# A hybrid decoder layer on one core: convolution taps, sample products and the scaling of x put on the vector engine, and one evacuation and sigmoid moved up

## The chip, the core and the metric

The kernel runs on one core of a Trainium2 chip. The core has a matrix engine (TensorE, PE in the profile, with its weight loads shown as PEld), a vector engine (VectorE, DVE), a scalar engine (ScalarE, ACT), a general engine (GpSimd, POOL) and a queue engine that starts transfers (SyncE, SP). Each engine runs its own instructions in program order and waits on semaphores for the others. The metric is the device time of one execution in microseconds (us).

## The reference

One inference step of a one-layer decoder over 1024 prompt positions and 8 x 8 sample positions, width 1024, in float32. All 1088 positions go through the same layer, laid out with channels on the 128 partitions and positions along the free dimension.

```python
h = rmsnorm(x, norm_mix_pre)
(a_b, a_c, a_u, b_p, c_q, c_f, c_i, c_g, d_a, d_g) = split(h @ w_in, 10)   # ten blocks of 256 channels
ya = a_b * conv3(a_c * a_u)                       # A: short causal convolution
yb = scale * W_grp(mean_w(b_p) - b_p)             # B: trailing means over 2, 4, 8, 16 positions
yc = headnorm(hgrn2(c_q, c_f, c_i)) * silu(c_g)   # C: gated recurrence, done in chunks
u  = d_a * sigmoid(d_g)                           # D: gate, then a causal convolution of width 31
yd = silu(layernorm(conv31(u) + conf_b))
x  = x + rmsnorm(concat(ya, yb, yc, yd) @ w_out)
x  = x + rmsnorm(swiglu(rmsnorm(x)))
```

The kernel also returns the updated states of the four mixers. For the prompt the convolutions begin with zeros, for the samples with a given state.

## The kernel before, in words

**Products in split precision.** Every float32 operand of a product is split into a high part (a cast) and a low part (the rest): `XH[k]`, `XL[k]` for the activations, two halves of a tile `wop` for the weights. Each product is three products: high by high, low by high and high by low. `split_w` (lines 137 to 140) makes the cast on ACT (L139) and the rest on DVE (a `TT` at L65).

**Units.** `h @ w_in` is done in 20 units of 128 output columns. One unit is 8 slices k of the width by 3 products by 3 column chunks `CH` of 256, 384 and 448 positions, so 72 matmuls; its result lies in 3 of the 6 banks of PSUM. Line 203 gives the order of the units: `UNITS = (12, 10, 8, 18, 16, 13, 19, 11, 9, 17, 4, 2, 6, 0, 5, 3, 7, 1, 14, 15)`. `U0` to `U4` are the first five.

**The opening (lines 254 to 340)** is written out by hand for ACT, DVE and PE. Units 12, 10 and 8 (`U0`, `U1`, `U2`) run on x that is not yet divided by its root mean square, while the squares for that root are summed. The reciprocal roots are spread over the partitions into the tile `rb0` (L298). Then the loop of lines 324 to 335 rewrites the eight slices of x: `scale_x(k)` scales slice k by the gain and `rb0` and casts it into `XH[k]`, and `low_x(k)` makes `XL[k]`. For k = 6 and 7 the multiplication with `rb0` is done by POOL (lines 322 and 323); for the others by one DVE instruction (`STT`, L71). In the same loop stand `prep_half(U3, ...)`, which splits the weights of unit 18, and `evac_r(U1)` and `evac_r(U2)`, which multiply the results of units 10 and 8 with `rb0` on their way out of PSUM. Unit 18 needs the three banks of unit 10. `HF[0]` is the forget gate of mixer C for the first 128 channels; its sigmoid stands at line 339, behind the loop.

**The planned part (lines 345 to 1128).** From unit 18 on a planner in Python writes the instruction order of PE and DVE; the order of ACT, POOL and SP is left to the compiler's scheduler. `unit` yields after 4 or 8 matmuls, `drive` turns that into a budget (0.1135 per matmul), and `hook` spends it on generators that yield what they cost: first the handlers of finished units (`first`), then the recurrence of mixer C (`crit`, function `hgrn`), then the rest (`bulk`). A generator that yields nothing is passed over for that time. Tiles are counted out with `take` and `give` (`z` and `u` have two buffers each). At the start of unit 18 the budget is set to -12.

**The wide convolution.** `d_gate` and `d_val` make u; `d_conv(j)` convolves channels 128 j to 128 j + 127. For the 64 sample positions it multiplies windows of u with the 31 taps on POOL, four products for each of two halves `q`, and sums them with a DVE reduction (L529). For the 1024 prompt positions 21 taps are multiply-adds on DVE (L71, `y<-u,taps,y` in the profile; the first is a `tensor_scalar`). The other 10 (`OFF`) are products on ACT (L540, `y<-u,taps`) into staging tiles, each of which but the first is added to `acc` by a transfer that accumulates (L542, `y<-y`), started from POOL. At the end DVE adds `acc` (line 551). `a_c`, the short convolution, and `b_pool`, the pooling, use tiles that the staging also uses, and wait for `("acc", j)`.

**Behind it.** `d_fin` does the layer norm of mixer D after both `d_conv`. `put_y` writes the mixers' outputs into `XH` and `XL` while the last unit runs, mixer D's first. Then come the output projection (`project`, matmuls at L1189), the feed-forward part (L1461 and others) and the outputs.

Of the kernel before, what the change touches and what calls it, by code (L numbers as in the profile page):

```python
# [12 lines left out]
AF = mybir.ActivationFunctionType  # L13
ALU = mybir.AluOpType
# [4 lines left out]
SEQ = 1024  # L19
# [33 lines left out]
def body(ctx, tc, xT, win, wout, wgu, wdn, par, con, msk, poolw, s_conv, s_pool, s_hgrn, s_conf,  # L53
         yT, o_conv_p, o_pool_p, o_hgrn_p, o_conf_p, o_conv_s, o_pool_s, o_hgrn_s, o_conf_s, hd, hx):
    nc = tc.nc
    V, S, PE, GP, SY = nc.vector, nc.scalar, nc.tensor, nc.gpsimd, nc.sync
# [7 lines left out]
    def TT(out, a, b, op=ALU.mult, eng=None):  # L64
        (eng or V).tensor_tensor(out, a, b, op)  # L65
# [4 lines left out]
    def STT(out, a, s, b, op0=ALU.mult, op1=ALU.add, eng=None):  # L70
        (eng or V).scalar_tensor_tensor(out=out, in0=a, scalar=s, in1=b, op0=op0, op1=op1)  # L71

    def f32(ap):
        return ap.bitcast(F32)
# [15 lines left out]
    def pc(name, i):  # L90
        return prm[:, PCOL[name] + i:PCOL[name] + i + 1]
# [6 lines left out]
    XH = [T(xp, [P, NT], f"xh{k}", F32R) for k in range(KT)]  # L98
    XL = [T(xp, [P, NT], f"xl{k}", F32R) for k in range(KT)]
# [70 lines left out]
    ys = [T(yp, [P, NT], f"y{k}") for k in range(KT)]  # L170
# [76 lines left out]
    def prep_half(n, h):  # L247
        hl = T(wp, [P, 2, 4 * P], "wop", F32R).rearrange("p w (k c) -> p w k c", c=P)
        split_w(wraw[n][h], hl)
        wq.setdefault(n, []).append(hl)  # L250
# [3 lines left out]
    with tc.manual_schedule(engines={mybir.EngineType.Activation, mybir.EngineType.DVE, mybir.EngineType.PE}):  # L254
        sq = {}
        pu[U0], pu[U1] = banks(), banks()

        def square(k):
            sq[k] = ht(NT)
            S.activation(sq[k], ys[k], AF.Square)  # L260
            if k:
                TT(sq[0], sq[0], sq[k], ALU.add)

        prep_half(U0, 0)
        for k in range(KT):
            split_x(k, pc("g_mix", k), CH if k == 0 else [(0, NT)])
            if k == 1:
                prep_half(U0, 1)
            if k in (2, 5):
                prep_half(U1, k // 5)  # L270
            if k >= 1:
                square(k - 1)
            mm_unit(U0, k)
            if k >= 3:
                mm_unit(U1, k - 3)
        square(KT - 1)
        zv.append(zt())
        for c, (o, n) in enumerate(CH):
            S.copy(zv[0][:, o:o + n], pu[U0][c][:, :n])
        st = sm()  # L280
        V.memset(st[64:, 8:9], 1.0)
        for i, (go, gn) in enumerate(GRP):
            PE.matmul(st[:gn, i:i + 1], sq[0][:, go:go + gn], ones[:, :1], start=True, stop=True, skip_group_check=True)
        mm_unit(U1, 5)
        for r0 in rsqrt_steps(st[:, :9], [P, 9], 1.0 / D, "x"):
            pass
        prep_half(U2, 0)
        prep_half(U2, 1)
        load_unit(U3)
        mm_unit(U1, 6)  # L290
        pu[U2] = banks()
        rb0 = ht(NT)
        for c, (o, n) in enumerate(CH):
            ps = sm()
            for i, (go, gn) in enumerate(GRP):
                if o <= go < o + n:
                    bcast(ps, r0[:, i:i + 1], gn, go - o)
            S.copy(rb0[:, o:o + n], ps[:, :n])  # L298
            if c == 1:
                mm_unit(U1, 7)  # L300
        mm_unit(U2, *range(KT))

        def scale_x(k):
            if k >= 6:
                S.activation(XH[k], ys[k], AF.Copy, scale=pc("g_mix", k))
            else:
                STT(ys[k], ys[k], pc("g_mix", k), rb0, ALU.mult, ALU.mult)
                S.copy(XH[k], ys[k])

        def low_x(k):  # L310
            if k >= 6:
                STT(XL[k], ys[k], pc("g_mix", k), f32(XH[k]), ALU.mult, ALU.subtract)
            else:
                TT(XL[k], ys[k], f32(XH[k]), ALU.subtract)

        def evac_r(n):
            t = ht()
            for c, (o, w) in enumerate(CH):
                TT(t[:, o:o + w], pu[n][c][:, :w], rb0[:, o:o + w])
            return t  # L320

        for k in (6, 7):
            TT(ys[k], ys[k], rb0, eng=GP)
        for k in range(KT):
            scale_x(k)
            if k >= 1:
                low_x(k - 1)
            if k in (1, 2):
                prep_half(U3, k - 1)
            if k == 3:  # L330
                HF[0] = evac_r(U1)
            if k == 4:
                load_unit(U4)
            if k == 6:
                HQ[0] = evac_r(U2)
        low_x(KT - 1)
        prep_half(U4, 0)
        prep_half(U4, 1)
        S.activation(HF[0], HF[0], AF.Sigmoid)
        S.activation(HQ[0], HQ[0], AF.Silu)  # L340


# [77 lines left out]
    done = set()  # L420

    def after(name):
        while name not in done:
            yield None

    def wait(n=1):
        for _ in range(n):
            yield None
# [51 lines left out]

    sg, uu = {}, {}
    US = 30 + SEQ
    OFF = 10

    def d_gate(j, ps):
        yield from take(z=1)
# [27 lines left out]
    def d_conv(j):  # L514
        u = uu[j]
        y = ys[6 + j]
        us = u[:, US:].rearrange("p (b t) -> p b t", t=38)
        dwj = taps[:, 31 * j:31 * (j + 1)]
        dwb = dwj.unsqueeze(1).unsqueeze(1).to_broadcast([P, 1, 8, 31])
        for q in range(2):  # L520
            yield from take(z=1)
            t = zt([P, 4 * 8, 31])
            for b in range(4):
                seg = us[:, q * 4 + b, :]
                win_ap = bass.AP(seg.tensor, seg.offset, [list(seg.ap[0]), [1, 8], [1, 31]])
                TT(t[:, b * 8:(b + 1) * 8], win_ap, dwb[:, 0], eng=GP)
            yield from wait(5)
            r = T(const, [P, 32], "cr")
            V.tensor_reduce(r, t, AX.X, ALU.add)  # L529
            TS(y[:, SEQ + 32 * q:SEQ + 32 * (q + 1)], r, pc("cb", j), 0.0, ALU.add, ALU.add)  # L530
            give(z=1)
            yield 1.4

        acc, *stage = [ys[i][:, :SEQ] for i in ((0, 1, 2) if j == 0 else (3, 5))]
        own = 31 - OFF
        for w in range(31):
            i = w // 2
            if w % 2 == 0 and i < OFF:
                dst = stage[i % len(stage)] if i else acc
                S.activation(dst, u[:, own + i:own + i + SEQ], AF.Copy, scale=dwj[:, own + i:own + i + 1])  # L540
                if i:
                    GP.dma_start(acc, dst, accum_op=ALU.add)  # L542
            if w >= own:
                continue
            if w == 0:
                TS(y[:, :SEQ], u[:, 0:SEQ], dwj[:, 0:1], pc("cb", j))
            else:
                STT(y[:, :SEQ], u[:, w:w + SEQ], dwj[:, w:w + 1], y[:, :SEQ])
            yield 1.2
        yield from wait(2 * LW)  # L550
        TT(y[:, :SEQ], y[:, :SEQ], acc, ALU.add)
        done.add(("acc", j))
        yield 1.2
        give(u=1)
        done.add(("conv", j))

# [47 lines left out]
        give(mm=3)  # L604

    def a_c(j, ps):
        yield from after(("acc", 0))
        while j not in zu:
            yield from wait(LW)
        yield from take(u=1)  # L610
        cu = ut(2 + SEQ + NB * 10)
        z = zu[j]
        cs = cu[:, 2 + SEQ:].rearrange("p (b t) -> p b t", t=10)
        GP.memset(cu[:, 0:2], 0.0)
        SY.dma_start(cs[:, :, 0:2], s_conv[j])
        yield from wait(LW)
        for (o, n), q in pchunks(ps):
            TT(cu[:, 2 + o:2 + o + n], q, z[:, o:o + n])
            yield 0.5
        TT(cs[:, :, 2:10], sample(ps), z[:, SEQ:].rearrange("p (b t) -> p b t", t=8))  # L620
        give(mm=3, z=1)
        SY.dma_start(o_conv_p[j], cu[:, SEQ:SEQ + 2])
        SY.dma_start(o_conv_s[j], cs[:, :, 8:10])
        y = ys[j]
        yb = y[:, SEQ:].rearrange("p (b t) -> p b t", t=8)
        for w in range(3):
            cw = pc("conv_w", 3 * j + w)
            if w == 0:
                S.activation(y[:, :SEQ], cu[:, 0:SEQ], AF.Copy, scale=cw)
                S.activation(yb, cs[:, :, 0:8], AF.Copy, scale=cw)  # L630
                yield from wait(LW)
            else:
                STT(y[:, :SEQ], cu[:, w:w + SEQ], cw, y[:, :SEQ])
                STT(yb, cs[:, :, w:w + 8], cw, yb)
                yield 1.4
        give(u=1)
        done.add(("conv a", j))
# [25 lines left out]
        bulk.insert(0, b_pool(j, p, s))  # L663

    def b_pool(j, p, s):
        yield from after(("acc", j))
        yield from wait(2 * LW)
        yield from take(h=2)

# [1281 lines left out]
```

## Time and profile before

| | us |
|---|---|
| runs | 1214.53, 1216.1, 1218.18 (median 1216.1) |
| the profiled execution, its own time | 1219.45 |
| its span in the profile | 1217.7 |
| PE busy | 1161.2 |
| DVE busy | 882.5 |
| ACT busy | 477.3 |
| POOL busy | 139.4 |

The span runs from the first to the last recorded instruction. A busy time is a sum over the whole span, which has stages with different limits: the opening, the planned part to about 381 us, and the projection and feed-forward parts behind it. The list of waits tells for each engine and line how long it sat idle and what ended that; a time given there for an engine that is not needed soon costs nothing. The tables by window give the busy time of each engine in a stretch, and as PEclk the clock granted to PE as a share of its full speed.

### The profile page before, as it was taken

The numbers are of one execution on the slowest core, as the hardware profiler recorded it, in microseconds if no ns is written. First come the engines' busy times: TensorE is split into PE (matmuls) and PEld (weight loads), VectorE is DVE, ScalarE is ACT, GpSimd is POOL, SyncE is SP. The second block draws the span as 40 slices with busy tenths as digits, with TensorE's granted clock in tenths as the row PEclk, the third lists the DMA queues.
The fourth block names the chain that finished last, engine by engine and source line by source line (L and its number), as shares of the span: only waits on it lengthen the run. The fifth ranks groups of instructions, "written<-read, shape, count | busy, mean of one in ns | idle before, by whom it ended". The sixth has DMA issues, their size and how long they took to land.

```text
span 1217.7 us, 21870 instructions
## 1 busy us (share of the span) xinstructions
PE 1161.2 (95%) x8435; PEld 1126.5 (93%) x8435; DVE 882.5 (72%) x1791; ACT 477.3 (39%) x1013; POOL 139.4 (11%) x206
## 2 busy tenths in 40 slices
PE   7899898599999999999999999999999999999995
PEld 6788888599899999999999999999999999999995
DVE  7775597379747567878766777877867558888666
ACT  7264532335226445343333444443433542222321
POOL 1202102200000000000000000000000332337323
PEclk9899899799979999999999999999999999999997
DMA  7116414630205412303313435533544678863555
GB/s 256 35 35 126 87 35 93 123 64 19 45 23 168 156 38 73 129 24 101 117 58 105 138 102 175 172 113 121 181 157 125 206 234 255 265 186 107 163 105 95
DMA packets 106057, 146.35 MB, mean 120 GB/s; under 512 B 25312, under 2 KB 72672, under 8 KB 105952
## 3 DMA queue, kind: packets, MB, share of 16 engines
q1 hardware_dynamic: 95008, 108.71, 28.9%
q0 software_dynamic: 10944, 36.25, 12.5%
q8 instruction: 66, 1.08, 0.4%
q14 instruction: 39, 0.32, 0.1%
HBM read 94.90 MB, written 40.57 MB: 111 GB/s over the span
## 4 chain that ended last, share of the span: by engine, by line
PE 80%; DMA 8%; DVE 6%; issue 2%; ACT 2%; POOL 1%; SPq 0%; ACTq 0%; POOLq 0%; DVEq 0%
PE p L1461 30%; PE p L1694 14%; PE mm L1052 11%; PE p L1189 8%; DMA y<-y 6%; PE p L1571 6%; PE p L1370 6%; PE mm L146 2%; DVE y L71 2%; PE sm L866 1%; DVE wop L65 1%; DMA raw<-wgu 1%; PE sm L437 1%; PE p L1155 0%; DMA y<-xT 0%
## 5 line engine op out<-in xcount | busy, mean ns | idle before, releaser
L65 DVE TENSOR_TENSOR wop<-raw,wop 128x512 fp32r<-128x512 f32 (+2 forms) x296 | 196.0, 675 | 98.7 <-ACT wop L1075 91.6
L1075 ACT CAST wop<-raw 128x512 fp32r<-128x512 f32 (+1 forms) x240 | 141.9, 604 | 244.3 <-DVE raw L65 115.8
L1461 PE MATMUL p<-xh,wop 128*128 128x272 f32 x1216 | 235.6, 289 | 1.7 <-DVE c L65 1.7
L1461 PEld LDWEIGHTS p<-xh,wop 128*128 128x128 f32 x1216 | 193.1, 188 | 1.9 <-DVE c L65 1.9
L1052 PE MATMUL mm<-xh,wop 128*128 128x256 f32 (+2 forms) x816 | 177.3, 346 | 16.1 <-ACT z L477 11.0
L1461 PE MATMUL p<-t,wop 128*128 128x272 f32 x912 | 177.2, 288 | 0.0
L1461 PE MATMUL p<-xl,wop 128*128 128x272 f32 x608 | 175.0, 288 | 0.0
L1052 PEld LDWEIGHTS mm<-xh,wop 128*128 128x128 f32 x816 | 137.3, 198 | 23.8 <-ACT z L477 11.4
L1461 PEld LDWEIGHTS p<-t,wop 128*128 128x128 f32 x912 | 144.7, 188 | 0.0
L1461 PE MATMUL p<-x,wop 128*128 128x272 f32 x456 | 130.5, 286 | 0.0
L1461 PEld LDWEIGHTS p<-xl,wop 128*128 128x128 f32 x608 | 114.6, 188 | 0.0
L1189 PE MATMUL p<-xh,wop 128*128 128x272 f32 x512 | 99.1, 290 | 0.0
L1052 PE MATMUL mm<-xl,wop 128*128 128x256 f32 (+2 forms) x408 | 97.6, 349 | 0.0
L1461 PEld LDWEIGHTS p<-x,wop 128*128 128x128 f32 x456 | 85.8, 188 | 0.0
L1694 PE MATMUL p<-xh,wop 128*128 128x272 f32 x456 | 82.0, 288 | 0.0
L1694 PE MATMUL p<-xl,wop 128*128 128x272 f32 x456 | 81.4, 288 | 0.0
L1189 PEld LDWEIGHTS p<-xh,wop 128*128 128x128 f32 x512 | 81.0, 188 | 0.0
L65 DVE TENSOR_TENSOR raw<-raw,raw 128x512 f32<-128x512 f32 (+1 forms) x123 | 71.2, 589 | 11.4 <-DMA raw<-wgu 8.7
L65 POOL TENSOR_TENSOR x<-raw,x 128x544 fp32r<-128x544 f32 (+3 forms) x6 | 7.5, 1246 | 605.5 <-ACT x L1619 575.1
L1189 PE MATMUL p<-xl,wop 128*128 128x272 f32 x256 | 74.0, 289 | 2.0 <-DVE xl L65 2.0
L1370 PE MATMUL p<-xh,wop 128*128 128x272 f32 x384 | 74.1, 289 | 0.0
L1052 PEld LDWEIGHTS mm<-xl,wop 128*128 128x128 f32 x408 | 69.6, 200 | 3.2 <-issue 0.4
(317 smaller groups left out, 2141.4 us busy)
## 6 DMA issues: line engine op xcount, KB each, us to landing
raw<-wgu SPq DMA_DIRECT2D x88, 256.0 KB, 3.4
hx<-hi SPq DMA_DIRECT2D x84, 136.0 KB, 2.5
raw<-win SPq DMA_DIRECT2D x40, 256.0 KB, 3.6
y<-y POOLq DMA_DIRECT2D x18, 512.0 KB, 4.8
hx<-x SPq DMA_DIRECT2D x64, 136.0 KB, 2.8
raw<-wdn SPq DMA_DIRECT2D x32, 256.0 KB, 3.3
xh<-hx POOLq DMA_DIRECT2D x15, 544.0 KB, 5.5
xl<-hx POOLq DMA_DIRECT2D x15, 544.0 KB, 5.2
```

The source lines that it names most:

```text
L65: (eng or V).tensor_tensor(out, a, b, op)
L71: (eng or V).scalar_tensor_tensor(out=out, in0=a, scalar=s, in1=b, op0=op0, op1=op1)
L146: PE.matmul(ps[c][:, :n], hl[:, wi, kk], X[k][:, o:o + n], start=k == 0 and wi == 0 and X is XH, stop=k == KT - 1 and wi == 1)
L437: PE.matmul(st[:, i * w:(i + 1) * w], sq[:, go:go + P], ones[:, :1] if rhs is None else rhs, start=True, stop=True, skip_group_check=True)
L866: PE.matmul(ps[:rows, g * P:(g + 1) * P], kk[:, o:o + rows], qz[hf][:, :, g * 64:(g + 1) * 64], start=True, stop=True, skip_group_check=True)
L1052: PE.matmul(ps[c][:, :w], hl[:, wi, kk], X[k][:, o:o + w], start=k == order[0] and wi == 0 and X is XH, stop=k == order[-1] and wi == 1)
L1075: S.copy(hl[:, 0], raw)
L1189: PE.matmul(ps[nt][:, :PW], WO[nt][k // 4][:, wi, kk:kk + P], X[k][:, o:o + PW], start=k == korder[0] and wi == 0 and X is XH, stop=k == k ...
L1370: PE.matmul(ps[r][:, :PW], w[:, wi, (k % 4) * P:(k % 4 + 1) * P], X[k][:, o:o + PW], start=k == 0 and wi == 0 and X is XH, stop=k == KT - ...
L1461: PE.matmul(ps[:, :PW], wop[:, wi, kk * P:(kk + 1) * P], x(kk, xi), start=first and kk == 0 and wi == 0 and xi == 0, stop=kk == 3 and wi == 1,
L1571: PE.matmul(ps[:, :n], wd[:, wi, kk * P:(kk + 1) * P], hops[k][xi][:, o:o + n], start=first and kk == 0 and wi == 0 and xi == 0, stop=not ...
L1694: PE.matmul(ps[:, :PW], ws[name][wi][q], x[:, xi, pr], start=first and q == 0 and wi == 0 and xi == 0, stop=q == 1 and wi == 1, skip_group ...
```

## The change

Three parts. (1) All eight slices of x are scaled by DVE from `rb0`; POOL's two multiplications go. (2) `evac_r(U1)` follows the second scaling instead of the fourth, the two `prep_half(U3, ...)` follow the third and fourth scaling instead of the second and third, and the sigmoid of `HF[0]` follows the fifth scaling instead of standing behind the loop. (3) In `d_conv` the sample products are done by DVE, the wait between them and their reduction goes, and all 31 taps are DVE instructions; `acc`, its staging tiles, its transfers and the waits on `("acc", j)` go.

```diff
         def scale_x(k):
-            if k >= 6:
-                S.activation(XH[k], ys[k], AF.Copy, scale=pc("g_mix", k))
-            else:
-                STT(ys[k], ys[k], pc("g_mix", k), rb0, ALU.mult, ALU.mult)
-                S.copy(XH[k], ys[k])
+            STT(ys[k], ys[k], pc("g_mix", k), rb0, ALU.mult, ALU.mult)
+            S.copy(XH[k], ys[k])
 
         def low_x(k):
-            if k >= 6:
-                STT(XL[k], ys[k], pc("g_mix", k), f32(XH[k]), ALU.mult, ALU.subtract)
-            else:
-                TT(XL[k], ys[k], f32(XH[k]), ALU.subtract)
+            TT(XL[k], ys[k], f32(XH[k]), ALU.subtract)
...
-        for k in (6, 7):
-            TT(ys[k], ys[k], rb0, eng=GP)
         for k in range(KT):
             scale_x(k)
             if k >= 1:
                 low_x(k - 1)
-            if k in (1, 2):
-                prep_half(U3, k - 1)
-            if k == 3:
+            if k == 1:
                 HF[0] = evac_r(U1)
+            if k == 4:
+                S.activation(HF[0], HF[0], AF.Sigmoid)
+            if k in (2, 3):
+                prep_half(U3, k - 2)
             if k == 4:
                 load_unit(U4)
...
-        S.activation(HF[0], HF[0], AF.Sigmoid)
         S.activation(HQ[0], HQ[0], AF.Silu)
...
     US = 30 + SEQ
-    OFF = 10
...
-                TT(t[:, b * 8:(b + 1) * 8], win_ap, dwb[:, 0], eng=GP)
-            yield from wait(5)
+                TT(t[:, b * 8:(b + 1) * 8], win_ap, dwb[:, 0])
             r = T(const, [P, 32], "cr")
             V.tensor_reduce(r, t, AX.X, ALU.add)
             TS(y[:, SEQ + 32 * q:SEQ + 32 * (q + 1)], r, pc("cb", j), 0.0, ALU.add, ALU.add)
             give(z=1)
-            yield 1.4
-
-        acc, *stage = [ys[i][:, :SEQ] for i in ((0, 1, 2) if j == 0 else (3, 5))]
-        own = 31 - OFF
+            yield 2.6
         for w in range(31):
-            i = w // 2
-            if w % 2 == 0 and i < OFF:
-                dst = stage[i % len(stage)] if i else acc
-                S.activation(dst, u[:, own + i:own + i + SEQ], AF.Copy, scale=dwj[:, own + i:own + i + 1])
-                if i:
-                    GP.dma_start(acc, dst, accum_op=ALU.add)
-            if w >= own:
-                continue
             if w == 0:
                 TS(y[:, :SEQ], u[:, 0:SEQ], dwj[:, 0:1], pc("cb", j))
             else:
                 STT(y[:, :SEQ], u[:, w:w + SEQ], dwj[:, w:w + 1], y[:, :SEQ])
             yield 1.2
-        yield from wait(2 * LW)
-        TT(y[:, :SEQ], y[:, :SEQ], acc, ALU.add)
-        done.add(("acc", j))
-        yield 1.2
         give(u=1)
...
     def a_c(j, ps):
-        yield from after(("acc", 0))
...
     def b_pool(j, p, s):
-        yield from after(("acc", j))
```

## The prediction

> **What bounds the kernel now.** I read the page first, for the share of each engine and the chain that ended last.
>
> ```profile
> PE 1161.2 (95%) x8435; PEld 1126.5 (93%) x8435; DVE 882.5 (72%) x1791; ACT 477.3 (39%) x1013; POOL 139.4 (11%) x206
> PE 80%; DMA 8%; DVE 6%; issue 2%; ACT 2%; POOL 1%; SPq 0%; ACTq 0%; POOLq 0%; DVEq 0%
> PE p L1461 30%; PE p L1694 14%; PE mm L1052 11%; PE p L1189 8%; DMA y<-y 6%; PE p L1571 6%; PE p L1370 6%; PE mm L146 2%; DVE y L71 2%; PE sm L866 1%; DVE wop L65 1%; DMA raw<-wgu 1%; PE sm L437 1%; PE p L1155 0%; DMA y<-xT 0%
> ```
>
> PE holds four fifths of the chain. The one large share that is not PE is `y<-y`, 6%: the transfers that add ACT's taps to `acc`. The change touches only the stage from 41.49 us (first scaling) to 381 us (projection), so next I asked for the waits in that stage, all engines first, then PE alone.
>
> ```profile
> ACT y L540 <- DMA y<-y: 64.7, 15, 7.3
> PE mm L1052 <- ACT z L477: 11.0, 1, 11.0
> PE sm L866 <- ACT vtok L748: 5.2, 1, 5.2
> PE mm L1052 <- DVE h L65: 5.0, 1, 5.0
> PE sm L866 <- ACT qz L838: 4.2, 1, 4.2
> PE sm L866 <- issue: 2.4, 1, 2.4
> PE sm L800 <- DVE h L71: 2.1, 1, 2.1
> ```
>
> The columns are total, times, longest. ACT waits 64.7 us for the accumulating transfers, in fifteen pieces. That alone would cost nothing. The lines below it show that it does: PE three times waits for an ACT instruction of another kind. The order of ACT and the chain of waits say why.
>
> ```profile
> 94.06 5.09 DMA y<-y
> 217.38 1.15 ACT L540 ACTIVATE y<-u,taps 128x1024 f32<-128x1024 f32 x1 [4.37 <-DMA y<-y]
> 220.62 1.19 ACT L477 ACTIVATE z<-mm 128x256 f32<-128x256 f32 x3
> 238.55 1.15 ACT L540 ACTIVATE y<-u,taps 128x1024 f32<-128x1024 f32 x1 [5.83 <-DMA y<-y]
> 239.60 0.57 ACT L748 COPY vtok<-sm 128x512 f32<-128x512 f32 x1
> 66.87 1.28 ACT L339 ACT_TABLE_LOAD   x1
> ```
>
> A tap on ACT needs its staging tile back, so it waits for a 5 us transfer, and whatever stands behind it waits too. At 220.62 that is the evacuation of a unit, without which PE has no bank; at 239.60 a copy for the next transposes. The same holds for the wait of 4.2 and, by its place behind a tap, for the 2.4 that the profile gives to issue. The 5.0 is another matter: unit 18 waits in the opening for unit 10's banks. The windows of 5 us give the clock after these waits.
>
> ```profile
> 55.00:60.00 5.00, 2.14 (x6) 1.68 (x7) 5.00 (x7) 1.10 (x1) 0.00 (x0) 0.80 0.16 52
> 85.00:90.00 5.00, 5.00 (x27) 4.70 (x24) 4.61 (x6) 0.38 (x1) 0.00 (x0) 0.66 0.00 0
> 110.00:115.00 5.00, 3.02 (x17) 3.05 (x17) 0.71 (x1) 2.65 (x5) 0.86 (x1) 0.76 0.72 168
> 135.00:140.00 5.00, 5.00 (x22) 4.90 (x22) 2.70 (x6) 3.95 (x14) 0.87 (x1) 0.51 0.55 105
> 220.00:225.00 5.00, 3.95 (x12) 3.70 (x13) 2.22 (x5) 3.31 (x7) 0.09 (x1) 0.50 0.70 108
> 240.00:245.00 5.00, 4.78 (x20) 4.74 (x21) 0.62 (x5) 0.17 (x1) 0.88 (x1) 0.50 0.90 208
> 245.00:250.00 5.00, 5.00 (x22) 4.67 (x21) 4.79 (x13) 2.20 (x4) 0.88 (x1) 0.59 0.03 7
> 335.00:340.00 5.00, 5.00 (x21) 4.87 (x21) 4.66 (x15) 0.00 (x0) 0.00 (x0) 0.50 0.15 26
> ```
>
> Columns are the length, then PE, PEld, DVE, ACT and POOL busy, then the clock. Slow work after a wait costs busy time times (1 - clock). After the four waits behind ACT's taps: 3.02 x 0.24 + 5.00 x 0.49 + 3.95 x 0.50 + 4.78 x 0.50 + 5.00 x 0.41 = 9.6 us. After the wait of 2.1: 5.00 x 0.34 = 1.7.
>
> Last, DVE, which takes over the work: how full it is.
>
> ```profile
> 41.49:335.00 293.51, 263.41 (x1635) 239.67 (x1634) 213.49 (x320) 119.32 (x248) 34.99 (x42) 0.94 0.32 67
> 335.00:381.00 46.00, 44.01 (x232) 40.61 (x231) 28.12 (x62) 21.19 (x34) 0.00 (x0) 0.82 0.14 40
> 140.00:200.00 60.00, 60.00 (x413) 54.44 (x413) 53.09 (x79) 23.81 (x59) 5.88 (x7) 1.00 0.18 44
> 175.00:200.00 25.00, 25.00 (x179) 22.82 (x179) 22.79 (x40) 6.51 (x14) 5.88 (x7) 1.00 0.25 50
> ```
>
> To 335 us it is busy 213.49 of 293.51, 73%. Where taps are at hand and nothing stalls it is 88% (140 to 200) or 91% (175 to 200), with PE full. So there is room, but not much.
>
> **The change part by part.** The rows for the prices:
>
> ```profile
> 41.49 7.29 DVE L71 SCALAR_TENSOR_TENSOR y<-y,prm,h 128x1088 f32<-128x1088 f32 x2 [4.43 <-ACT h L298]
> 41.54 6.09 POOL L65 TENSOR_TENSOR y<-y,h 128x1088 f32<-128x1088 f32 x2 [37.25 <-ACT h L298]
> 51.14 1.34 DVE L71 SCALAR_TENSOR_TENSOR y<-y,prm,h 128x1088 f32<-128x1088 f32 x1
> 52.40 1.28 DVE L65 TENSOR_TENSOR xl<-y,xh 128x1088 fp32r<-128x1088 f32 x1
> 54.22 0.69 DVE L65 TENSOR_TENSOR wop<-raw,wop 128x512 fp32r<-128x512 f32 x1 [0.54 <-ACT wop L139]
> 57.29 1.42 DVE L65 TENSOR_TENSOR h<-mm,h 128x256 f32<-128x256 f32 x3
> 57.86 16.86 PE mm L1052 x90
> 233.71 2.59 DVE L65 TENSOR_TENSOR tot<-h 128x272 f32<-128x272 f32 x1
> L71 DVE SCALAR_TENSOR_TENSOR y<-u,taps,y 128x1024 f32<-128x1024 f32 x40 | 51.3, 1282 | 0.9
> L65 DVE TENSOR_TENSOR y<-y,y 128x1024 f32<-128x1024 f32 x2 | 2.4, 1222 | 0.0
> L65 DVE TENSOR_TENSOR u<-mm,z 128x256 f32<-128x256 f32 x4 | 1.6, 412 | 10.7 <-ACT z L477 10.6
> ```
>
> *Opening.* While POOL makes its two products (6.09), DVE's first two scalings take 7.29 instead of 2 x 1.34 = 2.7. Without POOL that is 4.6 saved; two scalings more cost 2.7. Starts lie 1.26 apart after a scaling, about 1.2 after a low part. New order on DVE from 41.49: two scalings, a low part, the evacuation (1.33): done at 46.5. A scaling, a low part, a wait for ACT's cast (0.54) and the first weight half (0.65): 50.2. PE comes free at 57.86 - 5.0 = 52.8, so it begins unit 18 then. But the low parts set the pace at the end: five scalings, six low parts, the other half (1.2) and the second evacuation put the last one at 66.2. Unit 18 then ends about 67.3. Before, the row of 90 matmuls holds this unit and 18 of the next; at 16.86 / 90 less the slow start, some 0.164 each, it ended at 57.86 + 16.86 - 2.9 = 71.8. **Gain 4.3 us**, less than the wait. The sigmoid and its table load put about 1.28 + 1.15 (as long as a pass over 1024 columns) in front of the sixth cast on ACT. That cast's low part comes behind one more scaling, so it is hidden; without that cover, 1.2. The weights of unit 16 load behind unit 18's halves on SP and are used after 66: hidden.
>
> The wait of 2.1 and its 1.7 of clock come because DVE started the recurrence late, after sigmoid and two scalings on ACT. Those move up by 2 to 4, PE by 4: it may stay or go, 0 to 3.8; I take **1.9**.
>
> *Taps off ACT.* 20 products and 18 transfers go, with POOL's 18 issues; no DMA is added. Gone with them: waits of 11.0 + 5.2 + 4.2 + 2.4 = **22.8** and their **9.6** of clock, of which I take 9. Nothing else stands ahead of those ACT instructions but work that runs when its input is there.
>
> By the Trainium skill, TensorE: Matmul & The Clock Gate, Part 1, PE falls to half clock after an idle window of about 3.4 us and recovers after one busy window. By that, three of these four waits would cost 1.7 each, an estimate of 5.1 where the rows give 9.6. The trace agrees on the half clock but differs on its end: 335 to 340 runs at 0.50 with PE busy throughout. So the rows stand.
>
> *Work onto DVE.* 20 taps x 1.282 = 25.6. 16 sample products of 248 columns: at the nearest row (0.412 for 256) 6.6. Their windows overlap, which no DVE row shows; from below I bound them by the columns, 6.4, from above by twice the row, 13.2, which at 91% busy would take 7 off the gain. Two adds of `acc` go, -2.4. POOL's sample products go, beside which a 272-wide product took 2.59 for some 0.4: -2.2 for that one alone. With the opening: 25.6 + 6.6 - 2.4 - 2.2 + 2.7 - 4.6 = +25.7, so to 335 us 239.2 instead of 213.5.
>
> *Waits that go in the planner.* Sample products and reduction now follow at once, so the taps can begin when u is there; before, the reductions sat in DVE's order between steps of the recurrence that ACT held up. More taps stand in DVE's queue ahead of recurrence steps, each at most 1.28.
>
> *Sum.* If PE sets the pace: 4.3 + 1.9 + 22.8 + 9 = 38 saved, so 255.5 us for that stretch, and DVE at 239.2 / 255.5 = 94%. That is more than the best stretch shows. At 91.2% DVE needs 262.3, a gain of 31; at 88.5%, 270.3, a gain of 23. I take **27**: the profiled execution of 1219.45 (span 1217.7) becomes 1192, and the median of 1216.1 becomes **1189**. All behind 381 us moves up unchanged, since PE is full there.
>
> **The rivals.**
>
> *DVE holds back more.* The recurrence waits on PE and ACT at every step, and after 70 us there is a stretch without taps to fill with. At 85% DVE needs 281.4, a gain of 12: 1204. For it: 140 to 200 is a stretch full of taps, and the mean is 73%. Against: the emptiness of today comes from ACT's stalls.
>
> *Slower.* DVE becomes the bound of the stage: its queue is in order, taps stand ahead of recurrence steps, PE waits for those. It decides below 239.2 / 293.5 = 81.5% busy. At 78% the stretch takes 306.7, 13 more: 1229. Against it: with taps in the order, PE stayed at 60.00 of 60. The Trainium skill, Perfetto Trace Analysis, Identifying the Most-Contended Engine, says to relieve the engine with the highest occupancy first; the page of this profile has DVE at 72% and ACT at 39%, so the rule speaks against loading DVE, though the waits above put the stall on the less busy engine.
>
> *It doesn't do what it says.* The stalls pass to other ACT or DVE work of the same steps and only the opening's 4 remain, given back at the tail, where mixer D's norm comes later by its ten extra taps: no change, 1216. Against: no other ACT instruction waits for a transfer in such a way.
>
> **How the numbers follow.** My forecast (gain 20 to 42, so 1174 to 1196; 42 is the 38 with the other half of the 3.8 and some clock) has a chance of 0.6. DVE holding back more (gain 4 to 20, 1196 to 1212) has 0.2, no change 0.07, slower 0.13. From 1170 to 1208 lies about 0.77 to 0.8 of it. Faster by over 0.3% (3.6 us, what a measurement of this kernel tells from no change) is the first two, 0.8; within it 0.07; slower 0.13.
>
> **What the changed profile would show.** No `y<-y` transfers between 90 and 250 us, and none in the chain; PE's waits for ACT's z, vtok and qz gone or under 1 us; clock 1.00 where those slices stood at 0.5; unit 18 starting near 52.8 and the projection starting near 354 instead of 381; 60 taps at 1.28; DVE to the end of the stage near 90%. The prediction is wrong if PE waits for DVE lines in place of ACT lines, if the sample products take over 0.8 each, or if the tail between the last unit and the projection grows.

## The result, and the profile after

The changed kernel takes 1177.98 us (median of 4 runs, 1176.47 to 1179.85), the kernel before beside it 1215.87. The ratio is 0.9687, 95% interval 0.9667 to 0.9708: 37.9 us, or 3.1%, faster. The forecast was 1189 in a range of 1170 to 1208. The profiled execution took 1177.86, against 1219.45 before. The runs of the kernel before lie in two groups, near 1210 and near 1217 us, so its median differs from one set of runs to the next.

The page of the changed kernel, its engines and the head of its chain:

```profile
PE 1144.7 (97%) x8435; PEld 1110.9 (94%) x8435; DVE 902.9 (77%) x1827; ACT 456.1 (39%) x993; POOL 104.4 (9%) x170
PE 85%; DVE 9%; DMA 2%; ACT 2%; issue 1%; SPq 0%; POOL 0%; DVEq 0%; ACTq 0%; POOLq 0%
L71 DVE SCALAR_TENSOR_TENSOR y<-u,taps,y 128x1024 f32<-128x1024 f32 x60 | 76.9, 1282 | 1.4
```

DMA in the chain fell from 8% to 2%. DVE has 60 taps of 1.282, and its busy time over the span grew by 902.9 - 882.5 = 20.4. The list of PE's waits from 36 to 400 us (total, times, longest):

```profile
PE p L1163 <- DVE xl L65: 4.5, 5, 3.1
PE mm L1026 <- DVE xl L65: 2.7, 2, 2.0
PE sm L543 <- DVE s L65: 0.8, 1, 0.8
PE sm L787 <- DVE attn L779: 0.5, 2, 0.3
```

Before, four waits of 2.4 to 11.0 stood here behind ACT's taps. None is left. The longest are now the first low parts of the projection (3.1), which DVE makes, and the low parts in the opening (2.0). The windows show the same from the side of the clock (length, then PE, PEld, DVE, ACT, POOL busy, then the clock). The first two fences are the changed kernel: the slices of 5 us in which the clock was low (with 65 to 70 us, at 0.89, they are all), and two long stretches. The third is the kernel before. Its stretch, and the longer one of the changed kernel, run from the first scaling to the first matmul of the projection.

```profile
60.00:65.00 5.00, 2.96 (x13) 2.51 (x12) 5.00 (x6) 4.07 (x5) 0.00 (x0) 0.77 0.00 2
335.00:340.00 5.00, 4.12 (x15) 3.27 (x16) 5.00 (x8) 1.96 (x4) 0.00 (x0) 0.58 0.35 111
340.00:345.00 5.00, 5.00 (x33) 5.00 (x33) 2.38 (x4) 0.00 (x0) 0.00 (x0) 0.74 0.54 177
```

```profile
38.95:292.00 253.05, 248.27 (x1623) 227.44 (x1622) 229.53 (x352) 96.76 (x224) 0.53 (x6) 0.99 0.15 40
38.95:329.45 290.50, 284.88 (x1847) 260.10 (x1845) 251.37 (x406) 113.13 (x250) 0.53 (x6) 0.99 0.15 39
```

```profile
41.49:376.20 334.71, 304.61 (x1846) 277.90 (x1845) 237.05 (x374) 136.66 (x273) 34.99 (x42) 0.92 0.29 62
```

The stretch shrank from 334.71 to 290.50, by 44.2 us. PE's idle time in it went from 334.71 - 304.61 = 30.1 to 5.6, which is 24.5. Summing busy time times (1 - clock) over slices of 1 us, the loss to a slow clock went from 23.1 to 1.6, which is 21.5. What remains, PE's work at full clock, is 281.5 before and 283.3 after. So the gain of the stretch is idle time and slow clock of PE, in about equal parts. Of the 23.1 us of slow clock before, 8.5 lie at 334 to 352 us, behind no recorded wait; not every kernel has such a loss there (below). Two amounts lie outside the stretch: the first scaling began 2.5 earlier (41.49 to 38.95; it varied from 38.95 to 42.45 over the kernels run here, with the same code ahead of it), and from the projection's first matmul to the end the kernel takes 846.45 instead of 841.50, so 4.95 was given back, by the projection's waits for low parts and the half clock behind them. 44.21 + 2.54 - 4.95 = 41.80, the difference of the two spans (1217.7 and 1175.9).

### The profile page after: what moved, and what is told of

It reads as the page before. It is cut to its first block, busy times and chain, and to the rows that moved or that the text cites. A ratio compares the mean times of both kernels' runs of the same rounds, so it can differ in the third digit from the quotient of the medians.

```text
span 1175.9 us, 21811 instructions
## 1 busy us (share of the span) xinstructions
PE 1144.7 (97%) x8435; PEld 1110.9 (94%) x8435; DVE 902.9 (77%) x1827; ACT 456.1 (39%) x993; POOL 104.4 (9%) x170
## 4 chain that ended last, share of the span: by engine, by line
PE 85%; DVE 9%; DMA 2%; ACT 2%; issue 1%; SPq 0%; POOL 0%; DVEq 0%; ACTq 0%; POOLq 0%
PE p L1435 31%; PE p L1668 14%; PE mm L1026 12%; PE p L1163 8%; PE p L1545 6%; PE p L1344 6%; PE mm L146 2%; PE sm L840 2%; DVE y L71 1%; DVE xl L65 1%; DVE wop L65 1%; DMA raw<-wgu 1%; PE p L1129 1%; DVE raw L65 0%; PE sm L915 0%
## 5 line engine op out<-in xcount | busy, mean ns | idle before, releaser
L1026 PE MATMUL mm<-xh,wop 128*128 128x256 f32 (+2 forms) x816 | 169.1, 334 | 0.0
L1026 PEld LDWEIGHTS mm<-xh,wop 128*128 128x128 f32 x816 | 130.7, 189 | 6.1 <-issue 1.1
L1026 PE MATMUL mm<-xl,wop 128*128 128x256 f32 (+2 forms) x408 | 92.7, 335 | 2.7 <-DVE xl L65 2.7
L65 DVE TENSOR_TENSOR raw<-raw,raw 128x512 f32<-128x512 f32 (+1 forms) x123 | 71.2, 589 | 11.7 <-DMA raw<-wgu 9.1
L71 DVE SCALAR_TENSOR_TENSOR y<-u,taps,y 128x1024 f32<-128x1024 f32 x60 | 76.9, 1282 | 1.4
L65 DVE TENSOR_TENSOR t<-p,t 128x272 f32<-128x272 f32 (+3 forms) x138 | 60.4, 449 | 15.7 <-PE p L1668 7.9
```

The lines of the kernel that those rows point to most:

```text
L1026: PE.matmul(ps[c][:, :w], hl[:, wi, kk], X[k][:, o:o + w], start=k == order[0] and wi == 0 and X is XH, stop=k == order[-1] and wi == 1)
```

## Experiments: the parts of the change

For every kernel the time is the median of its runs, and the ratio is to the kernel before in the same set of runs (before: 1216.0, 1211.4 and 1216.4 in the three sets). The changed kernel was not run again in these sets, so a difference of a few us from it, or between kernels of different sets, is not sure.

**The opening alone** (all of parts 1 and 2 of the change, shown in part; the convolution as before):

```diff
+            STT(ys[k], ys[k], pc("g_mix", k), rb0, ALU.mult, ALU.mult)
...
-        for k in (6, 7):
-            TT(ys[k], ys[k], rb0, eng=GP)
...
     OFF = 10
```

> Only the opening is changed (all scalings of x on the vector engine, the gate's evacuation and sigmoid early); the convolution keeps its ten taps on ACT with accumulating transfers and its sample products on POOL. Theory (the opening is worth its own shortening, the rest is the transfers): unit 18 starts about 5 us earlier after the first scaling, ends about 4.3 earlier, 0 to 2 more from the recurrence's earlier start, so 1210 (1208 to 1213). Rival (what the opening saves is given back at the next stall behind a transfer): 1214 to 1217, with PE's waits for ACT's z, vtok and qz grown by the same few us.

1212.22, ratio 0.9967 (0.9942 to 0.9992), so 3.8 us by the medians, and 1 to 7 by the interval. The profiled execution is the fastest of its twelve, 1203.64. Its list of PE's waits:

```profile
PE mm L1045 <- ACT z L470: 11.1, 1, 11.1
PE sm L859 <- ACT qz L831: 9.1, 2, 4.9
PE sm L859 <- ACT vtok L741: 4.8, 1, 4.8
PE mm L1045 <- DVE xl L65: 2.7, 2, 2.0
```

The wait of 5.0 in the opening is down to 2.7 of smaller ones, but those behind ACT's taps stand. The wait for qz is here two, 4.9 and 4.2. In the list of before these were 4.2 and the 2.4 put down to issue, so they grew from 6.6 to 9.1: an earlier start is partly given back at the next stall. PE's idle time to the projection is 28.5, against 30.1 before. The half clock that stands at 334 to 352 us in the profile of before is missing in this execution, which may be why it is fast.

**The convolution alone** (opening as before):

```diff
+        for k in (6, 7):
+            TT(ys[k], ys[k], rb0, eng=GP)
...
+            if k == 3:
                 HF[0] = evac_r(U1)
```

> Only the wide convolution is changed (31 taps and the sample products on the vector engine, no transfers); the opening is the one of before. Theory: four waits of 22.8 us and 9 to 10 us of slow clock go, DVE has room, so 1183 to 1186. Rival (the two parts need each other: without the early opening DVE is late and becomes the bound): 1190 or more, with PE waiting for DVE lines in place of ACT lines.

1185.8, ratio 0.9759 (0.9731 to 0.9788). PE's waits now head with the opening's, and the one of 2.1 for the recurrence is there again:

```profile
PE mm L1033 <- DVE h L65: 4.4, 1, 4.4
PE p L1170 <- DVE xl L65: 3.7, 5, 3.1
PE sm L781 <- DVE h L71: 2.1, 1, 2.1
```

So the convolution carries 30 us, and the opening is worth 7.8 on top of it by the medians, against 3.8 alone. With the runs of one kernel 3 to 11 us apart, that it is worth more there is not shown.

**The opening's scaling on DVE, but its order as before:**

```diff
-            if k == 1:
+            if k in (1, 2):
+                prep_half(U3, k - 1)
+            if k == 3:
                 HF[0] = evac_r(U1)
-            if k == 4:
-                S.activation(HF[0], HF[0], AF.Sigmoid)
-            if k in (2, 3):
-                prep_half(U3, k - 2)
...
+        S.activation(HF[0], HF[0], AF.Sigmoid)
```

> The changed kernel with the opening's order put back (evacuation behind the fourth scaling, weight halves behind the second and third, sigmoid behind the loop), the scaling staying on DVE. Conv alone stood at 1185.8, conv and both parts of the opening at 1178.0. Theory A (the scaling without POOL carries the opening's gain): 1177 to 1180. Theory B (the order carries it, since unit 18 waits for that evacuation): 1182 to 1186, with a PE wait of 3 us or more at unit 18's start.

1186.53, ratio 0.9769 (0.9738 to 0.9799): no better than the convolution alone. The number is theory B's, its reason is not. Unit 18 does start early (first fence below: with a wait of 0.35, 11.7 behind the first scaling at 40.61; 11.2 in the changed kernel). What is late is mixer C's recurrence. Its first step on DVE waits for ACT's sigmoid and two scalings behind the loop, and starts 34.7 after the first scaling. In the changed kernel (second fence) it starts 23.7 after it.

```profile
52.30 1.38 PE L1025 MATMUL mm<-xh,wop 128*128 128x256 f32 x3 [0.35 <-DVE h L65]
75.29 0.73 DVE L68 TENSOR_SCALAR h<-h 128x1088 f32<-128x1088 f32 x1 [8.44 <-ACT h L737]
```

```profile
62.65 0.72 DVE L68 TENSOR_SCALAR h<-h 128x1088 f32<-128x1088 f32 x1
```

Its list of waits has PE waiting for that recurrence later on, as the kernel before did (2.1):

```profile
PE sm L773 <- DVE h L71: 2.7, 1, 2.7
```

So the scaling on DVE brings PE to unit 18 sooner by 4.7 us (before: 57.86 - 41.49 = 16.4), but by the medians that is lost again unless the order is changed too. What the trace shows late under the old order is the recurrence, behind the sigmoid. (The execution profiled is the fastest of its six, 1182.79.)

## Experiments: transfers, products and the sample wait

**ACT's ten products kept, no transfer** (DVE adds each product to `y` in place of the multiply-add; the waits on `("acc", j)` are back; shown in part):

```diff
+            if 0 <= nx < OFF:
+                S.activation(stage[nx % len(stage)], u[:, own + nx:own + nx + SEQ], AF.Copy, ...)
+            if i >= 0:
+                TT(y[:, :SEQ], y[:, :SEQ], stage[i % len(stage)], ALU.add)
```

> The changed kernel, but ten taps of each half are again products on ACT into staging tiles; each is added by a DVE add (1.22) instead of a multiply-add (1.28), and nothing is transferred. ACT has its 22.7 us of products back, DVE loses about 1. Theory (the wait for the transfers blocks ACT's queue, not its work): 1176 to 1181, no wait of PE for ACT over 1 us. Rival (ACT's own work stands in front of the evacuations): 1186 or more, with waits for ACT z or ACT qz back.

1179.72, ratio 0.971 (0.968 to 0.974), 1.7 above the changed kernel. ACT's work by itself costs next to nothing. What the transfers cost is not seen here, since this kernel also lacks the sample wait of before; a pair of kernels further down gives it.

**Few taps on ACT, with transfers**: 2 and 6 of the 31 in place of 0 (one and five transfers in each half). With them come back the add of `acc`, the planner's wait ahead of it and the waits on `("acc", j)`; everything else is as changed (shown in part):

```diff
+    OFF = 2        # the other kernel: 6
...
+                S.activation(dst, u[:, own + i:own + i + SEQ], AF.Copy, scale=dwj[:, own + i:own + i + 1])
+                if i:
+                    GP.dma_start(acc, dst, accum_op=ALU.add)
```

> The changed kernel with two taps of each half on ACT and one accumulating transfer each: no staging tile is used twice, so ACT never waits for a transfer, and DVE has two taps fewer and one add more (-1.3 each). Theory (only the wait for a staging tile costs): 1176 to 1180. Rival (each transfer costs some us by itself, through POOL or the adds that wait for it): 1182 or more.

> The changed kernel with 6 of the 31 taps of each half as products on ACT and five accumulating transfers each, sample products on DVE. Theory A (an ACT tap that waits for a transfer costs PE time only where PE's bank or transpose stands behind it, so the loss grows with their number): between the kernel with two such taps (1188) and the kernel with ten and the new opening (1212): 1190 to 1203, with an ACT wait for transfers of 25 to 35 us and at least one PE wait of 3 us for an ACT line. Theory B (only the ten together delay the recurrence): 1180 to 1190 and no such wait.

Two taps: 1188.45, ratio 0.9776 (0.9743 to 0.9808), 8 above what I expected. Six taps: 1183.91, ratio 0.9749 (0.9719 to 0.978), below two. So the loss does not grow with their number. For six taps both of theory A's signs are in the trace, ACT waits 25.4 for transfers and PE waits once behind it, but the time is theory B's.

```profile
ACT y L532 <- DMA y<-y: 25.4, 7, 4.9
PE sm L733 <- ACT vtok L740: 3.7, 1, 3.7
```

With two taps no ACT wait for a transfer shows. The windows of that kernel show something else:

```profile
295.00:300.00 5.00, 5.00 (x32) 4.21 (x31) 3.75 (x7) 2.16 (x6) 0.00 (x0) 1.00 0.01 2
300.00:305.00 5.00, 3.06 (x14) 1.92 (x11) 4.88 (x9) 0.29 (x2) 0.00 (x0) 0.75 0.27 47
305.00:310.00 5.00, 5.00 (x19) 4.74 (x18) 0.75 (x2) 0.49 (x1) 0.00 (x0) 0.50 0.34 111
315.00:320.00 5.00, 5.00 (x24) 4.92 (x23) 0.74 (x5) 0.00 (x0) 0.00 (x0) 0.50 0.00 0
```

PE stands still for 1.94 of 5 us behind DVE, and then runs at half clock from 302 to 323, in the stretch where short matmuls of one or two columns (the statistics of the mixers' norms) lie between the last unit's. By 1-us slices the slow clock takes 11.2 up to the projection, 9.5 of it here, against 1.6 in all in the changed kernel. That explains most of its 10 us, but not what keeps the clock down. One of this kernel's six runs took 1180.76, so the loss is not there in every execution. Nor does it need transfers: in the same stretch two kernels below that have none, with POOL's sample products and no wait and with mixer D's norm ahead of the pooling, lose 6.8 each, the one with six taps 5.1, the changed kernel nothing. What goes with it is a wait of PE. All six kernels whose profile has a wait of 1.6 to 1.9 for `s`, the state of the recurrence, near these matmuls lose 1.7 to 10 there. The changed kernel and three more (the opening alone, the order as before, the evacuation of unit 8 moved) wait 0.8 at most and lose nothing. It is not the whole cause: the convolution alone waits 0.8 and loses 1.7, and the kernel before loses 8.5 behind no wait.

**The same with the short matmuls spread out**, one for each step of the planner instead of three:

```diff
-            if i % SP == SP - 1:
-                yield None
+            yield None
```

> The kernel with two taps of each half on ACT, and the matmuls of the norm statistics (one or two columns wide) handed to PE one at a time between the unit's matmuls instead of three at a time. Theory (that kernel's 10 us over the changed kernel come from a clock at half speed while PE runs many narrow matmuls, 302 to 322 us, not from its two transfers): the slow stretch shrinks to under 5 us and the time falls to 1178 to 1183. Rival (the transfers and their adds cost it): 1186 to 1190 as without the spreading.

1190.39, ratio 0.9821 (0.9791 to 0.985). A miss: the slow clock still takes 10.1, now from 304 to 312 and 315 to 329. Handing them out in threes is not what keeps the clock down.

**The sample products**, in three kernels: on POOL with the planner's wait of 5 steps, on POOL without it, and on DVE with it. On POOL the cost told to the planner is 1.4 again, as before, in place of 2.6.

```diff
-                TT(t[:, b * 8:(b + 1) * 8], win_ap, dwb[:, 0])
+                TT(t[:, b * 8:(b + 1) * 8], win_ap, dwb[:, 0], eng=GP)   # on DVE in the third
+            yield from wait(5)                                           # left out in the second
```

> The changed kernel, but the sample products are on POOL again, with the wait of five turns before the reduction. All taps stay on the vector engine, without transfers. Theory (the sample products on the vector engine cost 5.6 of its time and save nothing on PE's path but a little contention): within 2 of the changed kernel, 1176 to 1180. Rival (the products beside POOL slow the vector engine, which is full, and taps begin later): 1181 to 1185.

> The changed kernel with the sample products on POOL, but no wait between them and their reduction. Theory A (late taps cost the 11 us): the taps begin within 8 us of the changed kernel's and the time is 1176 to 1182; DVE stands still some us at the reduction, which is ahead of steps of the recurrence. Theory B (POOL's products slow DVE): 1184 or more.

> The changed kernel with the planner's wait of 5 steps put back between the sample products and their reduction, the products staying on DVE. Theory A (the late start of the taps cost the kernel with POOL's sample products its 11 us): taps begin some 20 us later than in the changed kernel, and the time is 1184 to 1191. Theory B (POOL's own products, by slowing DVE beside them, cost it): 1176 to 1180, taps late or not.

| sample products | wait | us | ratio | first tap at |
|---|---|---|---|---|
| DVE (the change) | no | 1177.98 | 0.9687 (0.9667 to 0.9708) | 95.00 |
| POOL | no | 1188.93 | 0.9791 (0.9762 to 0.982) | 95.32 |
| POOL | yes | 1189.20 | 0.9815 (0.9787 to 0.9843) | 123.43 |
| DVE | yes | 1221.27 | 1.0053 (1.0031 to 1.0075) | 186.56 |

The kernel with POOL and the wait differs from the opening alone (1212.22) only in the taps: it has the same opening, the same sample products and the same wait, but no tap on ACT and no transfer. So taking the ten taps with their transfers off ACT is worth some 23 us there (18 by the ratios), and the sample products with their wait 11 more once that is done.

No theory holds for all three kernels. With the wait on POOL the taps end late, and that costs at the end of the stretch: the last tap starts at 321.3 instead of 276.4, and PE waits in front of the projection for mixer D's norm and the first cast of its outputs:

```profile
PE p L1164 <- ACT xh L1073: 4.5, 1, 4.5
PE sm L187 <- DVE rs_lny L71: 4.2, 1, 4.2
PE sm L430 <- DVE h L65: 3.8, 1, 3.8
```

On POOL without the wait the taps start as early as in the changed kernel, and 11 us are lost all the same. DVE's rows there, and one of PE, show how:

```profile
168.78 3.08 DVE L71 SCALAR_TENSOR_TENSOR y<-u,taps,y 128x1024 f32<-128x1024 f32 x2
171.78 2.28 DVE L65 TENSOR_TENSOR wop<-raw,wop 128x512 fp32r<-128x512 f32 x2
177.90 1.19 DVE L520 TENSOR_REDUCE cr<-z 128x32 f32<-128x992 f32 x1 [1.93 <-POOL z L65]
181.31 2.61 DVE L71 SCALAR_TENSOR_TENSOR y<-u,taps,y 128x1024 f32<-128x1024 f32 x2
183.95 1.33 DVE L779 COPY_PREDICATED attn<-mk,sm 128x512 f32<-128x512 uint32 x2
184.72 1.08 PE L958 MATMUL sm<-z,khat 64*64 64x512 f32 x4 [1.77 <-DVE attn L779]
```

Beside POOL's products (from 168.47 to 173.51) two taps take 3.08, elsewhere 2.61, and behind them two weight halves 2.28, elsewhere 1.28. The reduction waits 1.93 for POOL, with steps of the recurrence queued behind it and behind the taps that follow. PE waits 1.77 for `attn`; its clock is at half from 186 to 197, with another wait of 1.04 in between, some 5 us lost. Later it is at half from 295 to 302 and 309 to 316, 6.8 lost.

The wait with DVE products costs 43 us and makes the kernel slower than before, although no transfer is left in it. The products of the second four sample groups need one of the two `z` tiles. By the timeline ACT fills `z` tiles for other work at 95.76 and 109.83, and these products follow only at 180.50. That the lack of a tile held them up is read from this order, not tested. PE's rows show what came of it:

```profile
95.76 1.20 ACT L470 ACTIVATE z<-mm 128x256 f32<-128x256 f32 x3 [6.68 <-PE mm L1027]
109.83 1.20 ACT L470 ACTIVATE z<-mm 128x256 f32<-128x256 f32 x3 [0.84 <-PE mm L1027]
180.50 1.39 DVE L65 TENSOR_TENSOR z<-u,taps 128x248 f32<-128x248 f32 x4
210.43 0.65 PE L1027 MATMUL mm<-xh,wop 128*128 128x256 f32 x3
215.16 3.63 PE L841 MATMUL sm<-qz,h 128*112 128x128 f32 x16 [2.30 <-ACT qz L813]
253.34 1.25 PE L1027 MATMUL mm<-xh,wop 128*128 128x256 f32 x3
```

And the windows of the same kernel:

```profile
100.00:150.00 50.00, 49.42 (x340) 43.63 (x338) 19.12 (x44) 22.52 (x65) 0.00 (x0) 1.00 0.10 33
200.00:250.00 50.00, 35.21 (x190) 28.04 (x189) 47.48 (x62) 15.64 (x48) 0.10 (x1) 0.75 0.05 11
```

From 100 to 150 DVE is busy 19.12 of 50 and has no taps to fill with. From 200 to 250 it is full, with blocks of two to four taps between the steps of the recurrence. PE has no unit's matmuls from 210.43 to 253.34, only those steps, and waits between them. DVE's work came at the wrong time.

## Experiments: the tail and the opening's last waits

**Mixer D's norm ahead of the second pooling**, against the projection's wait, which is 4.5 in all in the changed kernel and was 2.0 by the page of before:

```profile
L1189 PE MATMUL p<-xl,wop 128*128 128x272 f32 x256 | 74.0, 289 | 2.0 <-DVE xl L65 2.0
```

```diff
-        bulk.insert(0, b_pool(j, p, s))
+        bulk.insert(0 if j == 0 else len(bulk), b_pool(j, p, s))
```

> The changed kernel, but the pooling of the second half stands behind mixer D's layer norm in the planner's list instead of ahead of it. Theory (the tail lost 5 us because the layer norm ends late: vector engine work ahead of the projection's first operands): the longest wait of PE in the projection, 3.1 us now, goes below 1.5 and its slow clock with it, so 1173 to 1176. Rival (the tail is set by the number of vector instructions after the last unit, not by their order): 1177 to 1179.

1181.61, ratio 0.9745 (0.9714 to 0.9777), slower than the changed kernel by some 3.6 by the medians. The projection's longest wait is still 3.0, and the clock is at half from 301 to 316 (6.8 us of slow clock in all). The theory fell: the order of the two does not set that wait.

**The evacuation of unit 8 behind the last low part**, against the opening's waits of 2.7:

```diff
-            if k == 6:
-                HQ[0] = evac_r(U2)
         low_x(KT - 1)
+        HQ[0] = evac_r(U2)
```

> The changed kernel, but the second evacuation of the opening (1.33 us on the vector engine) stands behind the last low part. Theory (in the opening PE waits 0.7 and 2.0 for low parts and then runs some 4 us at half clock, 1.6 lost): the low parts come 1.3 earlier, the waits fall by as much and the clock may stay, so 1175 to 1177. Rival (what is saved there is taken back by the vector engine's queue): 1177.5 to 1179.

1177.92, ratio 0.9717 (0.9689 to 0.9745), and the changed kernel has 1177.98. The opening's waits fell to 1.4 and its dip of the clock went, but no difference can be told in the time. None of these kernels is faster than the changed one by more than the spread of its runs.

## Why the prediction was right, and where its sizes were off

- **The waits behind ACT's taps (22.8).** All gone, as summed. PE's idle time fell by 24.5, with the opening's in it. With the opening alone they stay; with the taps off ACT too, and nothing else changed, some 23 us go. That the transfers and not ACT's products were the cost rests on the kernel that keeps the products at 1179.72, and on the trace of before, in which ACT waits for `y<-y` ahead of what PE waits for.
- **The step that failed: DVE gives 11 back.** The sum was 38 if PE sets the pace; 27 was taken since DVE would need 94%, "more than the best stretch shows". Nothing was given back: measured, 37.9 came. That this equals the 38 is chance, since the stretch gained 44.2 and the part behind it lost 5. DVE's work was over-sized: +25.7 forecast; 237.05 to 251.37 measured in the stretch, +14.3, which is 11.4 less. Over the whole span it is +20.4, so about 6 of it fell behind the start of the projection. By rows, each term named was right to about 1: the taps (76.9 - 51.3 = 25.6), the sample products (5.6 in place of 6.6, 0.35 each), the adds (-2.4), the 272-wide products (-2.1), the scalings (-2.0, by the sum 2.7 - 4.6). The rest, some 4, is spread over many rows that each fell by about 1 or less, and is not explained further. To 292 us DVE was busy 229.53 of 253.05, 90.7%, inside the 88 to 91% that the profile of before had shown, with PE full.
- **The clock (9).** Under-sized: 21.5 came back. By 1-us slices the four waits behind ACT's taps had cost 11.3 instead of 9.6. The sum left out the half clock at 334 to 352 us of the kernel before, though one of its slices is shown in the prediction; it had no wait ahead of it. That stretch is worth 8.5, and comes and goes between kernels and executions, so it is no sure gain. The execution of before that was profiled, 1219.45, also lies above the median of its runs.
- **Opening 4.3 and recurrence 1.9.** Together 6.2, where runs give 3.8 alone and 7.8 on top of the convolution. Unit 18 began 11.2 after the first scaling, 11.3 by the prediction. But its 72 matmuls ended some 28.1 after it, where 25.8 was forecast and it was 30.3 in the kernel before: PE waited 0.7 and 2.0 for low parts and lost 1.6 to the half clock behind them. So of the 4.3 about 2.2 came in this profile. The wait of 2.1 went, which puts the second term at the upper end of its 0 to 3.8.
- **The planner's waits, given no price.** This was the gap in the working. The taps start at 95.00 instead of 139.65. The sum held the sample products only as work for DVE (+6.6), but with their wait they are worth 11 us of the gain (1189.20 to 1177.98). Putting back the wait alone costs more than the whole gain with the products on DVE (1221), and nothing more with the products on POOL (1189 with and without it), so its price hangs on what else the planner hands out.
- **"The tail grows"** was named as a sign against the prediction. It came, at some 5 us: DVE's low parts for the projection, 2.0 before, hold PE 4.5. The gain ahead of it was far larger. So did "PE waits for DVE lines in place of ACT lines", in small: the waits that are left are for DVE, 8.5 in the list above. The projection begins at 329.45, 46.75 earlier than before, where 27 was forecast (its first matmul stands at 376.20 in the trace of before; the 381 of the prediction lies behind its first waits).
- **The rivals.** "DVE holds back more" and "slower" did not come about in the changed kernel, but the mechanism of the second is real: the kernel with the sample wait shows taps ahead of the recurrence and PE waiting for them.

Open: ten taps on ACT with their transfers but without the sample wait were not tried, so what the transfers cost is known only beside that wait (some 23 us). Why the half clock comes at 300 to 320 us in some orders, and lasts there, is not settled either.

## What to carry to other kernels

Look for an in-order engine that waits for slow transfers, and price what is queued behind it, not its own busy time. Moving that work to an engine that was already busier paid here, even with that engine 91% busy in the stretch with taps, since what PE lacked was the results on time. Where a planner hands out few buffers, a harmless wait while one is held can move a whole block of filler work, so price such waits as delays of what follows.

## What the runs showed of the hardware

- With POOL's products beside them the first two scalings on DVE took 7.29, without them 2.61 (row below, changed kernel): 3.65 against 1.31 each. In the kernel with the convolution alone, which also has POOL's products, two other instructions took that long: the two scalings 4.90 together, the low part behind them 3.63 instead of 1.28. By the Trainium skill, SBUF — State Buffer, Who interferes with whom, the two engines share a port pair under an exclusive lock; the trace agrees that they hinder each other.

```profile
38.95 2.61 DVE L71 SCALAR_TENSOR_TENSOR y<-y,prm,h 128x1088 f32<-128x1088 f32 x2 [2.84 <-ACT h L298]
```

- Half clock could last far longer than the gap before it. Behind 1.94 us of idle in 5, the kernel with two ACT taps ran 20 us slow, with PE busy 5.00 of 5.00 in slices at 0.50; behind a wait of 1.77, the one with POOL's sample products and no wait ran 11 us slow. Elsewhere it was short: in the kernel before, behind the opening's wait of 5.0 and the one of 2.4, the slow clock took 1.7 each, which is 3.4 us at half clock. The Trainium skill, TensorE: Matmul & The Clock Gate, Part 1, has the full clock back after one busy window of about 3.4 us; the two short stretches agree, the two long ones differ, and they decide here.
- PE's work at full clock in the stretch lay between 281.5 and 284.6 us in all the kernels. So all but about 3 us of the differences between them, 43 us from best to worst in the time, was PE's idle time, its slow clock, or the parts outside the stretch.
